# A diffusion trunk on one core: the opening's loads, norm and modulation in another order, and attention's columns and bias tables given out sooner

## The chip, the core and the metric

The kernel runs on one core of a Trainium2 chip. Five engines work side by side, each through its own instructions in order: TensorE (PE, matmuls; PEld is its loading of weights), VectorE (DVE), ScalarE (ACT), GpSimd (POOL) and SyncE (SP), which here only issues transfers. An engine waits where an instruction needs what another engine or a transfer has not yet delivered. The metric is the device time of one execution in microseconds.

## What is computed

Two layers over 512 tokens of width 1024. The first mixes by gated chunks and by neighbourhood attention with 256 context tokens, the second by a convolution; both end with a squared-ReLU MLP. Cut to what the change touches:

```python
sc_c = silu(c); sc_ctx = silu(c_ctx)
for l in range(2):
    m = sc_c @ w_mod[l] + b_mod[l]            # shift, scale, gain for both sub-layers
    sh1, s1, g1, sh2, s2, g2 = split(m, 6)
    h = rmsnorm(x, norm_g[l, 0]) * (1 + s1) + sh1
    if l == 0:
        hc = rmsnorm(ctx, norm_g[0, 0]) * (1 + cs1) + csh1
        z, q, k, v = split(h @ w_in)           # kc, vc from hc
        a = spatial_gating(z)
        b = softmax(q k^T / 8 + bias(rpb), masked) v     # 8 heads, windows of 8 x 16, and context
        y = concat(a, b) @ w_out
    else:
        y = conformer_conv(h)
    x = x + g1 * y
    x = x + g2 * square(relu((rmsnorm(x, norm_g[l, 1]) * (1 + s2) + sh2) @ w1)) @ w2
return rmsnorm(x, final_g)
```

## The kernel before

Activations are kept transposed, 1024 features as eight tiles of 128 x 512 tokens. Large matmuls are done three times in the short fp32r form, as high x high, low x high and high x low (L88, L89, L90, helper `mm3`); ACT casts the high half of each weight and VectorE or GpSimd subtracts to get the low half (`split`, L93 and L94). Results sit in eight PSUM banks that are handed round in order: a matmul into a bank waits until the last reader of that bank is done.

**Opening** (L250 to L500). SyncE issues every load in one queue: cc, four tiles of x (two feature blocks each, L256), vec, kon (L272), the modulation weights wmA (L266) and the first weight blocks raw (L120). ACT makes silu of c and squares eight blocks of x (L378), VectorE adds them one after another (L380), TensorE sums the last one over features in four narrow products (L386), ACT takes the root (L388), VectorE the reciprocal (L389), TensorE spreads it over all partitions (L392) and ACT copies it to r0 (L394). VectorE makes eight 128 x 128 diagonal blocks dgc from silu(c) (L400); TensorE multiplies them by ones (`silu_rows`, L404), and ACT copies the result to cB, the row that the columns below need. `mod_products(f)` for f = 0 to 3 gives shift and scale of two feature blocks each: eight products with wmA (L415), a copy ms (L420), a turn on TensorE (L424), and three small VectorE steps (L429 to L432). `modulate` then forms t = x · gain · r0 on VectorE (L350), the high half t + shift on ACT (L355), the low half on VectorE (L363). `first_operand(f)` calls it for two blocks, and takes a list of deferred low halves of the first weight (L136) to slip in after the first t. The products of the first q and k follow in `first_products`.

**Attention.** The 16 units u (four pairs of heads, four query blocks each) run two at a time: `scores` (three products per head, L831), `soften` (VectorE adds the bias table and finds the minimum, L844; ACT takes exp, L848), `turn` (TensorE turns the weights, L861; ACT copies them, L863) and, one round later, `weigh` (L877; at the last unit of a pair of heads also the sums, L885, the copy rs, L889, and yb, L891). Between these stand fill steps, `more(n)`: the products of values, projections and gate, with a weight piece split by ACT and GpSimd after each.

Beside them VectorE works through 24 columns: `gemv(j)` (L542) multiplies half of a 128 x 2048 tile graw with cB and sums it. The tile is one buffer with two halves, column j in half j mod 2; `early_load(j + 2)` (L527), called right behind column j, has SyncE fetch the half anew. `work(1)` takes one column, and is called four times in each round with u below 12. A bias table of a head is six VectorE additions (`head_bias`, L710) on a strip that `load_bias` fetches by two transfers (L698). The strips of two heads are fetched at the first round of a head pair, and their two tables made in its second round, after the first and third `work`. `turn_v` (L635 to L639) turns the values of one head pair; its two ACT copies vtok stand at the end of rounds 6 and 10. Where nothing else sets it, the order on each engine is that in which the code is written:

```python
        more(1)
        if u < 12:
            work(1)
        more(2)
        turn(u)
        if p_ < 3 and j == 2:
            head_bias(2 * p_ + 2, rows.pop(2 * p_ + 2))
```

Of the kernel before, what the change touches and what calls it, by code (L numbers as in the profile page):

```python
# [55 lines left out]
def body(ctx: ExitStack, tc: tile.TileContext, I: dict, out: bass.AP):  # L56
# [49 lines left out]
    class Weights:  # L106
# [16 lines left out]
        def piece(self, i, q, el=None):  # L123
# [11 lines left out]
            if isinstance(el, list):  # L135
                act.copy(hi.parts[q], src)  # L136
                el.append(lambda: dve.tensor_tensor(lo.parts[q], src, hi.parts[q].bitcast(F32), op=ALU.subtract))
            else:
                split(hi.parts[q], lo.parts[q], src, el=e)
# [113 lines left out]
    for k in range(0, KC, 2):  # L253
        t = mpa.tile([P, 2, 512], F32, tag="ablk", name=nm("x0"), bufs=6)
        x0 += [t[:, 0], t[:, 1]]
        sync.dma_start(t, I["xT"][:, k : k + 2, :])  # L256
# [7 lines left out]
    def load_wmA(i):  # L264
        w = graw() if i == 0 else sp.tile([P, 2048], F32, name=f"wmA{i}")
        sync.dma_start(w, I["wmA"][i])  # L266
        wmA.append(w.rearrange("p (k n) -> p k n", k=4))
# [4 lines left out]
    sync.dma_start(kon[:, :C_MASK], I["kon"][:, :C_MASK])  # L272
# [102 lines left out]
    before = None  # L375
    for k in range(KC):
        sq = slot(s="sq")
        act.activation(sq, x0[k], AF.Square)  # L378
        if k:
            dve.tensor_tensor(sq, sq, before, op=ALU.add)  # L380
        before = sq
    preload(AF.Sqrt)

    ps = bank()[:, :4]
    for n in range(4):
        pe.matmul(ps[:, n : n + 1], before[:, n * P : (n + 1) * P], ones[:, :1], start=True, stop=True)  # L386
    q = small(4, "q")
    act.activation(q, ps, AF.Sqrt, bias=epsc, scale=1.0 / D)  # L388
    dve.reciprocal(q, q)  # L389
    ps = bank()  # L390
    for n in range(4):
        pe.matmul(ps[:, n * P : (n + 1) * P], q[:, n : n + 1].to_broadcast([P, P]), ident, start=True, stop=True)  # L392
    r0 = slot(s="rstd")
    act.copy(r0, ps)  # L394


    cB = cp.tile([P, D], F32, name="cB")
    dgs = [slot(s="dgc") for _ in range(2)]
    for k in range(KC):
        dve.tensor_scalar(dgs[k // 4][:, k % 4 * P : k % 4 * P + P], ident, sc[:, k, 0:1], None, op0=ALU.mult)  # L400

    def silu_rows(i):
        ps = bank()
        pe.matmul(ps, ones, dgs[i], start=True, stop=True)  # L404
        return ps
# [44 lines left out]
    def first_operand(f, low=()):  # L450
        m = modulate([(x0[k], *colA(0, k), h[k][0], h[k][1]) for k in (2 * f, 2 * f + 1)], r0, lambda k: False)
        next(m)
        for go in low:
            go()
        run(m)

    pbs = {}
    pm = mod_products(0)
    next(pm)
    next(pm)  # L460
    next(pm)
    pbs[0] = silu_rows(0)
    run(pm)
    low = []
    W.piece(0, 0, low)
    first_operand(0, low)
# [7 lines left out]
    pbs[1] = silu_rows(1)  # L474
# [4 lines left out]
    for i in range(2):  # L479
        act.copy(cB[:, i * 512 : (i + 1) * 512], pbs[i])  # L480
# [38 lines left out]
    early = []  # L519

    def early_load(j):
# [3 lines left out]
        if j < 24:  # L525
            b = j % 2 * D
            sync.dma_start(early[0][:, b : b + D], I["wmB"][j // 2][:, b : b + D])  # L527
# [10 lines left out]
    def gemv(j):  # L538
# [6 lines left out]
        if j < 22:  # L545
            early_load(j + 2)
# [347 lines left out]
    rows = {hd: load_bias(hd) for hd in range(2)}  # L894
    for n, _ in enumerate(values(0, ctx_first)):
        if n in (6, 8):
            head_bias(n // 2 - 3, rows.pop(n // 2 - 3))
# [25 lines left out]
    def more(n):  # L923
        for _ in range(n):
# [3 lines left out]
            stage(begun)  # L928
            W.pieces(1, pool)


    NU = len(units)
    for u in range(0, NU, 2):
        p_, j = units[u]
        if p_ < 3 and j == 0:
            for e in range(2):
                rows[2 * p_ + 2 + e] = load_bias(2 * p_ + 2 + e)
# [6 lines left out]
        more(1)  # L944
        if u < 12:
            work(1)
        more(2)
        turn(u)
        if p_ < 3 and j == 2:
            head_bias(2 * p_ + 2, rows.pop(2 * p_ + 2))  # L950
        if u < 12:
            work(1)
        more(1)
        turn(u + 1)
        if u < 12:
# [634 lines left out]
```

## Time and profile before

| | us |
|---|---|
| time, median of 3 runs | 1176.74 (1176.14 to 1180.42) |
| the profiled execution | 1178.93 |
| its span in the trace | 1177.0 |
| of that, stretch 0 to 30: PE busy | 13.88 |
| stretch 30 to 75: PE busy | 44.25 of 45.00 |
| stretch 75 to 193 (attention): PE busy | 113.49 of 118.00, at a granted clock of 0.97 |
| stretch 193 to 1177: PE busy | 973.41 of 984.00 |

The profiled execution took 1.93 us more than its span, which runs from the first instruction to the last. Busy time of an engine is the time in which it executes; the granted clock is the share of full speed that TensorE was given. An idle stretch in the trace names what ended it, as in "<-DVE gn L728": the engine waited for the VectorE instruction of line 728 that writes gn.

### The profile page before, as it was taken

How to read it: one execution, taken by the hardware profiler on the slowest of the kernel's cores; microseconds unless marked ns; L12 is line 12 of the kernel's file. 1: busy time of each engine (PE TensorE's matmuls, PEld its weight loads, DVE VectorE, ACT ScalarE, POOL GpSimd, SP SyncE). 2: the span in 40 equal slices, each digit the busy share in tenths (PEclk: the TensorE clock that was granted, in tenths of full speed). 3: DMA queues.
4: the chain of work that ended last, by engine and by line, in shares of the span. 5: the costliest groups of instructions: out<-in, count | busy, mean ns of one | idle time of the engine just before them, and what ended most of it. 6: DMA issues, size and time to landing. Idle time of an engine off the chain costs nothing.

```text
span 1177.0 us, 16486 instructions
## 1 busy us (share of the span) xinstructions
PE 1145.0 (97%) x6574; PEld 954.9 (81%) x6574; DVE 722.1 (61%) x1247; ACT 472.2 (40%) x939; POOL 168.7 (14%) x162
## 2 busy tenths in 40 slices
PE   4999998999999999999999999999999999999997
PEld 2688897889888888888889766699988888888887
DVE  4666876658765665766667868577743443443445
ACT  4463555545532422423336232475632331341423
POOL 0142325552100000000023220043200000000001
PEclk9999998999999999999999999999999999999998
DMA  9525462242455455554531444304222332232322
GB/s 372 222 89 189 149 226 90 73 179 73 161 202 209 182 198 192 196 201 175 214 113 72 131 126 134 111 1 144 72 97 82 108 107 76 104 107 72 108 72 72
DMA packets 31468, 161.89 MB, mean 138 GB/s; under 512 B 4320, under 2 KB 7904, under 8 KB 15008
## 3 DMA queue, kind: packets, MB, share of 16 engines
q1 hardware_dynamic: 31392, 160.85, 39.2%
q8 instruction: 51, 0.84, 0.3%
q14 instruction: 25, 0.20, 0.1%
HBM read 152.52 MB, written 2.10 MB: 131 GB/s over the span
## 4 chain that ended last, share of the span: by engine, by line
PE 86%; DVE 6%; ACT 3%; DMA 3%; issue 1%; POOL 0%; SPq 0%; DVEq 0%; ACTq 0%; POOLq 0%
PE ps L88 22%; PE ps L89 22%; PE ps L90 22%; PE ps L218 3%; PE ps L215 3%; PE ps L216 3%; PE ps L1248 3%; DMA graw<-in_wmB_dram 2%; PE ps L877 1%; DVE graw L542 1%; PE ps L415 1%; DVE acc L325 1%; PE ps L831 1%; ACT s L848 1%; PE ps L861 1%
## 5 line engine op out<-in xcount | busy, mean ns | idle before, releaser
L93 ACT CAST whi<-raw 128x512 fp32r<-128x512 f32 x339 | 190.7, 616 | 197.7 <-PE ps L90 173.2
L88 PE MATMUL ps<-hhi,whi 128*128 128x512 f32 x640 | 251.7, 393 | 1.4 <-ACT hhi L355 1.4
L90 PE MATMUL ps<-hlo,whi 128*128 128x512 f32 x640 | 249.3, 390 | 0.4 <-DVE hlo L363 0.4
L89 PE MATMUL ps<-hhi,wlo 128*128 128x512 f32 x640 | 249.3, 390 | 0.2 <-DVE wlo L94 0.2
L94 DVE TENSOR_TENSOR wlo<-raw,whi 128x512 fp32r<-128x512 f32 x283 | 194.1, 723 | 36.8 <-ACT whi L93 35.9
L89 PE MATMUL ps<-hid,wlo 128*128 128x512 f32 (+1 forms) x520 | 196.3, 378 | 0.0
L90 PE MATMUL ps<-hid,whi 128*128 128x512 f32 (+1 forms) x520 | 196.3, 378 | 0.0
L88 PE MATMUL ps<-hid,whi 128*128 128x512 f32 (+1 forms) x520 | 196.3, 378 | 0.0
L998 DVE SCALAR_TENSOR_TENSOR x<-ps,mod,x 128x512 f32<-128x512 f32 (+1 forms) x94 | 62.7, 669 | 157.1 <-PE ps L90 148.0
L88 PEld LDWEIGHTS ps<-hhi,whi 128*128 128x128 f32 x640 | 120.2, 188 | 32.8 <-issue 6.1
L94 POOL TENSOR_TENSOR wlo<-raw,whi 128x512 fp32r<-128x512 f32 x56 | 81.9, 1479 | 427.0 <-ACT whi L93 426.8
L90 PEld LDWEIGHTS ps<-hlo,whi 128*128 128x128 f32 x640 | 120.1, 188 | 26.1 <-DVE hlo L363 0.9
L89 PEld LDWEIGHTS ps<-hhi,wlo 128*128 128x128 f32 x640 | 120.2, 188 | 24.4 <-DVE wlo L94 0.5
L542 DVE CUSTOM_DVE_ANT_0 graw<-graw,cB,vec 128x1024 f32<-128x1024 f32 x80 | 105.1, 1315 | 17.5 <-DMA graw<-in_wmB_dram 17.5
L88 PEld LDWEIGHTS ps<-hid,whi 128*128 128x128 f32 x520 | 97.8, 188 | 18.2
L90 PEld LDWEIGHTS ps<-hid,whi 128*128 128x128 f32 x520 | 97.8, 188 | 18.2
L89 PEld LDWEIGHTS ps<-hid,wlo 128*128 128x128 f32 x520 | 97.8, 188 | 18.0
L1124 DVE TENSOR_TENSOR z<-z 128x512 f32<-128x512 f32 (+1 forms) x72 | 46.4, 651 | 94.3 <-ACT z L1122 94.2
L1122 ACT ACTIVATE z<-ps 128x512 f32<-128x512 f32 (+1 forms) x72 | 38.9, 550 | 139.3 <-PE ps L90 136.7
L1128 DVE TENSOR_TENSOR hid<-z,hid 128x512 fp32r<-128x512 f32 (+1 forms) x72 | 45.7, 642 | 43.3 <-ACT hid L1126 43.3
L1126 ACT CAST hid<-z 128x512 fp32r<-128x512 f32 (+1 forms) x72 | 40.7, 573 | 51.8 <-DVE z L1124 51.8
L1478 POOL TENSOR_TENSOR o<-o,rstd 128x256 f32<-128x256 f32 x2 | 1.9, 952 | 322.2 <-DVE rstd L336 322.2
(260 smaller groups left out, 1680.1 us busy)
## 6 DMA issues: line engine op xcount, KB each, us to landing
raw<-in_w_ff_dram SPq DMA_DIRECT2D x64, 1024.0 KB
graw<-in_wmB_dram SPq DMA_DIRECT2D x28, 1024.0 KB
graw<-in_wmB_dram SPq DMA_DIRECT2D x24, 512.0 KB
raw<-in_w_pw_dram SPq DMA_DIRECT2D x12, 1024.0 KB
raw<-in_w_in_dram SPq DMA_DIRECT2D x10, 1024.0 KB
wmA<-in_wmA_dram SPq DMA_DIRECT2D x7, 1024.0 KB
y<-ypad SPq DMA_DIRECT2D x90, 67.5 KB
raw<-in_w_out_dram SPq DMA_DIRECT2D x4, 1024.0 KB
```

Source lines behind the costliest of these rows:

```text
L88: pe.matmul(ps, w[0], a[0], start=first, stop=False)
L89: pe.matmul(ps, w[1], a[0], start=False, stop=False)
L90: pe.matmul(ps, w[0], a[1], start=False, stop=last)
L93: (e or act.copy)(hi, src)
L94: (el or dve).tensor_tensor(lo, src, hi.bitcast(F32), op=ALU.subtract)
L215: pe.matmul(ps, w[0][:, k, c : c + P], a[0], start=n == 0, stop=False)
L542: dve.tensor_tensor_reduce(out=wv, in0=wv, in1=cB, scale=1.0, scalar=vcol(V_BMOD, l * 48 + q * 8 + j % 8), op0=ALU.mult, op1=ALU.add, accu ...
L998: dve.scalar_tensor_tensor(x[:, m, t0:t1], ps, gate[:, m : m + 1], x[:, m, t0:t1], op0=ALU.mult, op1=ALU.add)
L1122: act.activation(z, ps, AF.Relu)
L1124: dve.tensor_tensor(z, z, z, op=ALU.mult)
L1126: act.copy(hi, z)
L1128: dve.tensor_tensor(lo, z, hi.bitcast(F32), op=ALU.subtract)
```

## The change

In the opening, ACT's queue issues the second and fourth tile of x, kon and the second wmA; SyncE the rest. VectorE adds the squares in pairs only, and TensorE sums the four pairs over features into one bank, by products with a 128 x 128 matrix of ones, so that root and reciprocal are taken on all 128 partitions by 512 columns and no spreading is needed. GpSimd makes the eight dgc, both products with ones and the copies to cB come ahead of the first `mod_products`. x · r0 is formed ahead of the modulation (`scaled`), and ACT makes the high half from it with scale and shift in one step, VectorE the same in place and the low half from that. The deferral of the weight's low half goes.

In attention, the 24 columns stand as five in each of the rounds u = 0, 2, 4, 6 and four in u = 8, one after each fill step from the first on; u = 10 has none. The reload of a half is put on a list when its column is given out, and issued by ACT's queue after two more fill steps. One bias table is made in every round up to u = 10 (`next_bias`, after the third fill step), and the strip of the head two further on is fetched right behind it.

```diff
--- before.py
+++ after.py
@@ -132,11 +132,7 @@
             hi, lo = self.his[i]
             e = (dve, pool)[q % 2] if el == "both" else el
             src = self.raws[i][:, 2 * q : 2 * q + 2, :]
-            if isinstance(el, list):
-                act.copy(hi.parts[q], src)
-                el.append(lambda: dve.tensor_tensor(lo.parts[q], src, hi.parts[q].bitcast(F32), op=ALU.subtract))
-            else:
-                split(hi.parts[q], lo.parts[q], src, el=e)
+            split(hi.parts[q], lo.parts[q], src, el=e)
             self.cut += 1
             if q == 3:
                 del self.raws[i]
@@ -253,7 +249,7 @@
     for k in range(0, KC, 2):
         t = mpa.tile([P, 2, 512], F32, tag="ablk", name=nm("x0"), bufs=6)
         x0 += [t[:, 0], t[:, 1]]
-        sync.dma_start(t, I["xT"][:, k : k + 2, :])
+        (act if k % 4 else sync).dma_start(t, I["xT"][:, k : k + 2, :])
     st = ExitStack()
     sp = st.enter_context(tc.tile_pool(name="start", bufs=1))
     wmA = []
@@ -263,13 +259,13 @@
     def load_wmA(i):
         w = graw() if i == 0 else sp.tile([P, 2048], F32, name=f"wmA{i}")
-        sync.dma_start(w, I["wmA"][i])
+        (act if i == 1 else sync).dma_start(w, I["wmA"][i])
         wmA.append(w.rearrange("p (k n) -> p k n", k=4))
     vec = cp.tile([P, NV], F32, name="vec")
     sync.dma_start(vec, I["vec"])
     kon = cp.tile([P, NC_], F32, name="kon")
-    sync.dma_start(kon[:, :C_MASK], I["kon"][:, :C_MASK])
+    act.dma_start(kon[:, :C_MASK], I["kon"][:, :C_MASK])
     load_wmA(0)
     load_wmA(1)
     W.load()
@@ -372,37 +368,29 @@
     sc = blk(s="sc")[:, : KC * 32].rearrange("p (k m) -> p k m", m=32)
     act.activation(sc, cc, AF.Silu)
-    before = None
+    ss = SumSq()
+    ss.ps = bank()
+    dgs = [slot(s="dgc") for _ in range(2)]
     for k in range(KC):
         sq = slot(s="sq")
         act.activation(sq, x0[k], AF.Square)
-        if k:
+        if k % 2:
             dve.tensor_tensor(sq, sq, before, op=ALU.add)
+            pe.matmul(ss.ps, ones, sq, start=k == 1, stop=k == KC - 1)
         before = sq
+    cB = cp.tile([P, D], F32, name="cB")
+    for k in range(KC):
+        pool.tensor_scalar(dgs[k // 4][:, k % 4 * P : k % 4 * P + P], ident, sc[:, k, 0:1], None, op0=ALU.mult)
     preload(AF.Sqrt)
-    ps = bank()[:, :4]
-    for n in range(4):
-        pe.matmul(ps[:, n : n + 1], before[:, n * P : (n + 1) * P], ones[:, :1], start=True, stop=True)
-    q = small(4, "q")
-    act.activation(q, ps, AF.Sqrt, bias=epsc, scale=1.0 / D)
-    dve.reciprocal(q, q)
-    ps = bank()
-    for n in range(4):
-        pe.matmul(ps[:, n * P : (n + 1) * P], q[:, n : n + 1].to_broadcast([P, P]), ident, start=True, stop=True)
-    r0 = slot(s="rstd")
-    act.copy(r0, ps)
-    cB = cp.tile([P, D], F32, name="cB")
-    dgs = [slot(s="dgc") for _ in range(2)]
-    for k in range(KC):
-        dve.tensor_scalar(dgs[k // 4][:, k % 4 * P : k % 4 * P + P], ident, sc[:, k, 0:1], None, op0=ALU.mult)
-    def silu_rows(i):
+    r0 = ss.rstd(0, T)
+    pbs = []
+    for d in dgs:
         ps = bank()
-        pe.matmul(ps, ones, dgs[i], start=True, stop=True)
-        return ps
+        pe.matmul(ps, ones, d, start=True, stop=True)
+        pbs.append(ps)
+    for i in range(2):
+        act.copy(cB[:, i * 512 : (i + 1) * 512], pbs[i])
@@ -447,23 +435,25 @@
                 w, c = wqk[n // 2], (n % 2) * P
                 mm3(q0[n], (w[0][:, k, c : c + P], w[1][:, k, c : c + P]), h[k], k == 0, k == KC - 1)
-    def first_operand(f, low=()):
-        m = modulate([(x0[k], *colA(0, k), h[k][0], h[k][1]) for k in (2 * f, 2 * f + 1)], r0, lambda k: False)
-        next(m)
-        for go in low:
-            go()
-        run(m)
-    pbs = {}
+    def scaled(f):
+        for k in (2 * f, 2 * f + 1):
+            dve.tensor_tensor(x0[k], x0[k], r0, op=ALU.mult)
+    def first_operand(f):
+        for k in (2 * f, 2 * f + 1):
+            gs, sh = colA(0, k)
+            hi, lo = h[k]
+            act.activation(hi, x0[k], AF.Identity, scale=gs, bias=sh)
+            dve.tensor_scalar(x0[k], x0[k], gs, sh, op0=ALU.mult, op1=ALU.add)
+            dve.tensor_tensor(lo, x0[k], hi.bitcast(F32), op=ALU.subtract)
+        if f < 3:
+            scaled(f + 1)
+    scaled(0)
     pm = mod_products(0)
-    next(pm)
-    next(pm)
-    next(pm)
-    pbs[0] = silu_rows(0)
     run(pm)
-    low = []
-    W.piece(0, 0, low)
-    first_operand(0, low)
+    W.piece(0, 0)
+    first_operand(0)
     for q in range(1, 4):
         W.piece(0, q)
     wqk = {0: W.use()}
@@ -471,13 +461,10 @@
     pm = mod_products(1)
     next(pm)
     next(pm)
-    pbs[1] = silu_rows(1)
     next(pm)
     W.piece(1, 0)
     run(pm)
     first_operand(1)
-    for i in range(2):
-        act.copy(cB[:, i * 512 : (i + 1) * 512], pbs[i])
     for q in range(1, 4):
         W.piece(1, q)
     ctile = []
@@ -516,7 +503,7 @@
     gpool = [None, 12]
     gs_ = ExitStack()
-    early = []
+    early, soon = [], []
     def early_load(j):
@@ -524,7 +511,7 @@
             early.append(graw())
         if j < 24:
             b = j % 2 * D
-            sync.dma_start(early[0][:, b : b + D], I["wmB"][j // 2][:, b : b + D])
+            act.dma_start(early[0][:, b : b + D], I["wmB"][j // 2][:, b : b + D])
     def gemv_load(i):
         if i < 40:
@@ -543,7 +530,7 @@
             out=wv, in0=wv, in1=cB, scale=1.0, scalar=vcol(V_BMOD, l * 48 + q * 8 + j % 8),
             op0=ALU.mult, op1=ALU.add, accum_out=mods[(l, q)][:, j % 8 : j % 8 + 1])
         if j < 22:
-            early_load(j + 2)
+            soon.append([2, lambda: early_load(j + 2)])
         elif j == 23:
             gemv_load(gpool[1])
             gpool[1] += 1
@@ -892,9 +879,15 @@
             yb[p_] = b
     rows = {hd: load_bias(hd) for hd in range(2)}
+    def next_bias(hd):
+        head_bias(hd, rows.pop(hd))
+        if hd < 6:
+            rows[hd + 2] = load_bias(hd + 2)
     for n, _ in enumerate(values(0, ctx_first)):
         if n in (6, 8):
-            head_bias(n // 2 - 3, rows.pop(n // 2 - 3))
+            next_bias(n // 2 - 3)
         if n > 7:
             W.pieces(1, pool)
     early_load(0)
@@ -926,40 +919,34 @@
             if next(fill, 1) is None:
                 nfill[0] += 1
             stage(begun)
+            for due in list(soon):
+                due[0] -= 1
+                if due[0] == 0:
+                    due[1]()
+                    soon.remove(due)
             W.pieces(1, pool)
     NU = len(units)
+    columns = {0: 5, 2: 5, 4: 5, 6: 5, 8: 4}
     for u in range(0, NU, 2):
         p_, j = units[u]
-        if p_ < 3 and j == 0:
-            for e in range(2):
-                rows[2 * p_ + 2 + e] = load_bias(2 * p_ + 2 + e)
         left = [scores(u), scores(u + 1)]
         if u >= 2:
             weigh(u - 2)
             weigh(u - 1)
         left[0]()
         left[1]()
-        more(1)
-        if u < 12:
-            work(1)
-        more(2)
-        turn(u)
-        if p_ < 3 and j == 2:
-            head_bias(2 * p_ + 2, rows.pop(2 * p_ + 2))
-        if u < 12:
-            work(1)
-        more(1)
-        turn(u + 1)
-        if u < 12:
-            work(1)
-        if p_ < 3 and j == 2:
-            head_bias(2 * p_ + 3, rows.pop(2 * p_ + 3))
-        more(2)
-        if u < 12:
-            work(1)
-        more(1)
+        for n in range(7):
+            more(1)
+            if n == 2:
+                turn(u)
+            if n == 3:
+                turn(u + 1)
+            if n < columns.get(u, 0):
+                work(1)
+            if n == 2 and p_ < 3:
+                next_bias(2 * p_ + 2 + j // 2)
         if u in (6, 10):
             later.popleft()()
     weigh(NU - 2)
```

Three places show what this moves. Rows give line, operation, tiles and shape, and what is waited for (an engine's name stands for its semaphore, DMAHW for a transfer). First TensorE's beginning, before: sq are the squares, ps PSUM banks, graw and wmA the modulation weights.

```order
L386 MATMUL ps_142<-ones,sq_137 128x1 [waits DVE_49,Pool_49]
L386 MATMUL ps_142<-ones,sq_137 128x1 x3
L392 MATMUL ps_150<-kon,q_147 128x128 [waits DMAHW6_49,DVE_49]
L392 MATMUL ps_150<-kon,q_147 128x128 x3
L415 MATMUL ps_188<-graw_89,sc_115 32x512 [waits DMAHW7_49,Activation_49]
L415 MATMUL ps_188<-graw_89,sc_115 32x512 x3
L415 MATMUL ps_188<-wmA_91,sc_115 32x512 [waits DMAHW0_49]
L415 MATMUL ps_188<-wmA_91,sc_115 32x512 x3
L424 MATMUL ps_199<-kon,ms_197 128x128 [waits Activation_49]
L424 MATMUL ps_199<-kon,ms_197 128x128 x3
L404 MATMUL ps_204<-dgc_158,ones 128x512 [waits DVE_49]
```

And now:

```order
L379 MATMUL ps_117<-sq_122,ones 128x512 [waits DVE_49,Pool_49]
L379 MATMUL ps_117<-sq_128,ones 128x512 [waits DVE_49]
L379 MATMUL ps_117<-sq_134,ones 128x512 [waits DVE_49]
L379 MATMUL ps_117<-sq_140,ones 128x512 [waits DVE_49]
L390 MATMUL ps_158<-dgc_118,ones 128x512 [waits Pool_49]
L390 MATMUL ps_160<-dgc_119,ones 128x512 [waits Pool_49]
L403 MATMUL ps_186<-graw_89,sc_115 32x512 [waits DMAHW0_49,Activation_49]
L403 MATMUL ps_186<-graw_89,sc_115 32x512 x3
L403 MATMUL ps_186<-wmA_91,sc_115 32x512 [waits DMAHW7_49]
L403 MATMUL ps_186<-wmA_91,sc_115 32x512 x3
L412 MATMUL ps_197<-kon,ms_195 128x128 [waits DMAHW6_49,Activation_49]
L412 MATMUL ps_197<-kon,ms_195 128x128 x3
```

The four narrow sums and the spreading (L386, L392) have become four sums by 512 columns, and the two products with dgc, which stood behind the turn and in the second round, stand ahead of the first modulation product and wait for GpSimd.

Second, ACT's last rows of round u = 6, before: pt are turned attention weights, whi weight pieces, qt a projection, vtok the turned values, rs the spread sums.

```order
L863 COPY pt_1350<-ps_1345 128x512 [waits PE_49,Activation_49]
L863 COPY pt_1357<-ps_1352 128x512 [waits PE_49,Activation_49]
L93 CAST whi_1333<-raw_845 128x512
L863 COPY pt_1381<-ps_1376 128x512 [waits PE_49,Activation_49]
L863 COPY pt_1388<-ps_1383 128x512 [waits PE_49,Activation_49]
L583 ACTIVATE qt_1404<-ps_1326 128x8x8x8 [waits PE_49]
L93 CAST whi_1333<-raw_845 128x512
L638 COPY vtok_1428<-ps_1429 128x512 [waits PE_49]
L639 COPY vtok_1428<-ps_1430 128x384 [waits PE_49]
L889 COPY rs_1488<-ps_1479 128x512 [waits PE_49]
```

And now, with the transfers that ACT issues:

```order
L514 DMA graw_780<-in_wmB_dram 128x1024 [waits DMAHW2_49,DVE_49]
L93 CAST whi_1337<-raw_834 128x512
L850 COPY pt_1390<-ps_1385 128x512 [waits PE_49,Activation_49]
L850 COPY pt_1397<-ps_1392 128x512 [waits PE_49,Activation_49]
L570 ACTIVATE qt_1406<-ps_1330 128x8x8x8 [waits PE_49]
L514 DMA graw_780<-in_wmB_dram 128x1024 [waits DMAHW5_49,DVE_49]
L93 CAST whi_1337<-raw_834 128x512
L514 DMA graw_780<-in_wmB_dram 128x1024 [waits DMAHW6_49,DVE_49]
L514 DMA graw_780<-in_wmB_dram 128x1024 [waits DMAHW0_49,DVE_49]
L625 COPY vtok_1432<-ps_1433 128x512 [waits PE_49]
L626 COPY vtok_1432<-ps_1434 128x384 [waits PE_49]
L876 COPY rs_1486<-ps_1477 128x512 [waits PE_49]
```

Four of the five reloads of the round stand in these rows, and the last two directly ahead of the vtok copies, each waiting for a VectorE instruction, the column that frees the half.

Third, VectorE in round u = 10, before: gelu and gn belong to the gate, biases are the tables, graw the columns.

```order
L725 SCALAR_TENSOR_TENSOR gelu_1755<-gelu_1755,ps_1721 128x256 [waits Activation_49]
L710 TENSOR_TENSOR biases<-rows_1440,kon 128x128 [waits DMAHW2_49,DMAHW1_49]
L710 TENSOR_TENSOR biases<-rows_1440,kon 128x128 x5
L542 ISA graw_784,mod_414<-graw_784,cB,vec 128x1024 [waits DMAHW2_49]
L542 ISA mod_414 128x1
L728 SCALAR_TENSOR_TENSOR gn_1754<-gelu_1755,ps_1721 128x256 [waits Activation_49]
L761 BN_STATS bs_1795<-gn_1754 128x6 [waits DVE_49]
L762 BN_AGGR gmv<-bs_1795 128x2 [waits DVE_49]
L761 BN_STATS bs_1798<-gn_1754 128x6
L762 BN_AGGR gmv<-bs_1798 128x2 [waits DVE_49]
L856 RECIPROCAL tot_1446<-tot_1446 128x8
L542 ISA graw_784,mod_414<-graw_784,cB,vec 128x1024 [waits DMAHW4_49]
```

And now:

```order
L712 SCALAR_TENSOR_TENSOR gelu_1757<-gelu_1757,ps_1723 128x256 [waits Activation_49]
L697 TENSOR_TENSOR biases<-rows_1372,kon 128x128 [waits DMAHW4_49,DMAHW3_49]
L697 TENSOR_TENSOR biases<-rows_1372,kon 128x128 x5
L715 SCALAR_TENSOR_TENSOR gn_1756<-gelu_1757,ps_1723 128x256 [waits Activation_49]
L748 BN_STATS bs_1795<-gn_1756 128x6 [waits DVE_49]
L749 BN_AGGR gmv<-bs_1795 128x2 [waits DVE_49]
L748 BN_STATS bs_1798<-gn_1756 128x6
L749 BN_AGGR gmv<-bs_1798 128x2 [waits DVE_49]
L843 RECIPROCAL tot_1444<-tot_1444 128x8
L712 SCALAR_TENSOR_TENSOR gelu_1829<-gelu_1829,ps_1780 128x256 [waits Activation_49]
L715 SCALAR_TENSOR_TENSOR gn_1828<-gelu_1829,ps_1780 128x256 [waits Activation_49]
L748 BN_STATS bs_1834<-gn_1828 128x6 [waits DVE_49]
```

The columns are gone from this round, and of its two bias tables one is left.

## The prediction

> **What bounds the kernel now.** I read the page's busy times first, then TensorE's waits, then windows, then the chain and the timeline at the places found. Page, lines of busy time (share of the span, instructions); below it TensorE's waits (what waited, for whom: us in total, times, the longest):
>
> ```profile
> span 1177.0 us, 16486 instructions
> PE 1145.0 (97%) x6574; PEld 954.9 (81%) x6574; DVE 722.1 (61%) x1247; ACT 472.2 (40%) x939; POOL 168.7 (14%) x162
> PE ps L386 <- DVE sq L380: 13.0, 1, 13.0
> PE ps L831 <- DVE gn L728: 4.3, 1, 4.3
> PE ps L331 <- DVE acc L325: 1.5, 2, 0.9
> ```
>
> TensorE is the bound: 1177.0 − 1145.0 = 32 us are all that it is idle. Thirteen are the start and 4.3 are one wait in attention, so a change that leaves the matmuls alone works on some 20 us. Windows (start:end, length, then busy time and count on PE, PEld, DVE, ACT and POOL, granted clock, DMA share, GB/s):
>
> ```profile
> 0.00:10.00 10.00, 0.00 (x0) 0.00 (x0) 2.32 (x4) 5.14 (x8) 0.49 (x7) 1.00 0.80 268
> 10.00:20.00 10.00, 6.47 (x32) 4.16 (x32) 4.25 (x13) 3.49 (x6) 0.00 (x0) 1.00 1.02 428
> 181.00:188.00 7.00, 6.99 (x55) 6.07 (x56) 2.53 (x8) 1.87 (x6) 5.82 (x5) 0.54 0.47 154
> ```
>
> The third row shows a second cost of that one wait: the 7.00 us behind it ran at a granted clock of 0.54 with TensorE never idle, 7.00 × (1 − 0.54) = 3.2 us of work lost.
>
> **The stall in attention, which goes.** Timeline around it (start, duration, engine, line; in brackets idle before and its releaser; SPq is a DMA issue on SyncE's queue):
>
> ```profile
> 171.07 0.33 SPq L120 DMA_DIRECT2D raw<-in_w_in_dram  x1
> 171.49 2.77 SPq L527 DMA_DIRECT2D graw<-in_wmB_dram  x2
> 177.21 1.29 DVE L542 CUSTOM_DVE_ANT_0 graw<-graw,cB,vec 128x1024 f32<-128x1024 f32 x1 [1.95 <-DMA graw<-in_wmB_dram]
> 178.42 1.30 DVE L710 TENSOR_TENSOR biases<-rows,kon 128x128 f32<-128x128 f32 x6
> 180.54 0.42 DVE L728 SCALAR_TENSOR_TENSOR gn<-gelu,ps 128x256 f32<-128x256 f32 x1 [0.48 <-ACT gelu L727]
> 181.01 0.79 PE L831 MATMUL ps<-kh,q 64*128 64x512 f32 x1 [4.27 <-DVE gn L728]
> ```
>
> Read backwards: the scores wait for the bank that a gate product (L728) empties; VectorE does that late, behind a bias table and a column that waits 1.95 for its half, which SyncE issued behind a weight block. The new order puts no column into u = 10 and one bias table instead of two: columns (2 to 3 × 1.29), a bias (1.30) and the DMA wait (1.95) leave that row, 5.8 at least where 4.27 is needed. So the wait of 4.27 and the half clock of 3.2 go: **−7.5**. Late next there is the ready-made row of softmax work, which TensorE reaches with no wait in the pairs before; I cost it at 0.
>
> **The opening.** Chain of waits, in order of time (start, duration, step), and below it rows of the timeline and of groups (busy, mean ns):
>
> ```profile
> 12.13 0.70 DVE sq L380
> 17.45 3.25 PE ps L415 x16
> 20.72 0.59 ACT ms L420
> 21.36 0.67 PE ps L424 x4
> 22.05 0.20 DVE modA L429
> 24.76 0.67 DVE hlo L363
> 25.48 0.50 PE ps L90
> 28.08 1.90 PE ps L415 x16
> 10.12 1.15 ACT L378 ACTIVATE sq<-x 128x512 f32<-128x512 f32 x2 [0.17 <-DMA x<-in_xT_dram]
> 21.85 1.02 PE L404 MATMUL ps<-dgc,ones 128*128 128x512 f32 x2
> L336 DVE RECIPROCAL rstd<-rstd x8: 1753/1753/1754, 58.7 to 1160.1; 128x256 f32<-128x256 f32 x8
> L779 POOL TENSOR_SCALAR gn<-gn,gmv,gsd 128x128 f32<-128x128 f32 x8 | 6.3, 791 | 0.0
> L1213 DVE TENSOR_SCALAR zc<-ypad,vec 128x512 f32<-128x512 f32 x2 | 1.1, 539 | 0.0
> 136.34 6.10 POOL L94 TENSOR_TENSOR wlo<-raw,whi 128x512 fp32r<-128x512 f32 x4 [13.08 <-ACT whi L93]
> ```
>
> Two paths now meet at the first operand; both start when the squares are done. In the kernel before, two squares after the last tile end at 10.12 + 1.15 = 11.27 and the adds at 12.83. Now tiles 1 and 3 come by ACT's queue; the engines were 80% busy until 10 and more than full behind it, so tiles 2 and 3 land together at 10: four squares, 4 × 0.575, end at 12.3, one add (0.70) at 13.0. No gain there.
>
> Path one, 1/rms by 512 columns: the last sum 1.0 (the L404 row; up to 1.7 at the 3.25/1.90 that L415 shows cold over warm), root 0.6, reciprocal 2 × 1753 ns = 3.5, two products with x at 0.70: 13.0 + 1.0 + 0.6 + 3.5 + 1.4 = 19.5, 20.2 cold. Path two: GpSimd makes the eight dgc from the third add on, about 11.7. No row shows this operation there: the bounds per piece are 0.38 (L94, 6.10/16 blocks of 128 columns) and 0.79 (L779, same shape, two arithmetic steps where dgc has one); L779 is nearer by shape, L94 by steps, and I take the middle, 0.58: 11.7 + 4.7 = 16.4, second ones product 17.4, L403's eight products at 1.90 to 3.25, say 2.5: 19.9. Then, as in before, ms 0.59, turn 0.67, three small DVE steps of 0.20; then hi 0.58 on ACT, straight from x, DVE's 0.54 and 0.67: 3.7, and 0.3 for hand-overs: L90 at 23.9 against 25.48, a gain of 1.6. With 0.79 and 3.25 it is 26.4, a loss of 0.9; with 0.38 and 1.90 path one decides: 20.2 + 0.2 + 0.58 + 0.54 + 0.67 = 22.2, a gain of 3.3. The two cB copies and the weight's low half, which stood in the chain's holes, are still there and beside other work. The next operands lose a DVE product each (x · rstd is done ahead); of the 1.5 us waits at L331 I let 0.5 go. **−2.1**, between +0.9 and −3.8.
>
> The share of 0.80 up to 10 us leaves room the other way: 20% of 10 us were unused, and if a second queue filled them, x would land up to 2.0 us sooner and the opening give 4.1. Against it stands the same row: one queue alone reached 1.02 as soon as large tiles stood in it, so the engines and not the issue set the pace; I leave the 2.0 out. The Trainium skill, "DMA: Bandwidth & Descriptors", section "Issuing engines are not separate DMA queues", says that transfers run on the same 16 engines whichever engine starts them, and that a second issuer saves only sequencer time. By that rule the split tiles bring nothing and the sum stays at 1175.0; without it, it would be 1173.0.
>
> **The new wait.** Columns are five per pair in u = 0 to 6 instead of four, over the same two halves. ACT's queue now issues each half, two fill steps after the column that freed it. Timeline, queue and VectorE, then TensorE and ACT:
>
> ```profile
> 104.89 0.33 SPq L527 DMA_DIRECT2D graw<-in_wmB_dram  x1
> 108.61 1.28 DVE L542 CUSTOM_DVE_ANT_0 graw<-graw,cB,vec 128x1024 f32<-128x1024 f32 x1 [1.21 <-DMA graw<-in_wmB_dram]
> 109.82 3.47 DVE L710 TENSOR_TENSOR biases<-rows,kon 128x128 f32<-128x128 f32 x6
> 131.77 0.69 DVE L844 CUSTOM_DVE_ANT_1 s<-ps,biases 128x512 f32<-128x512 f32 x1
> 136.12 1.27 DVE L542 CUSTOM_DVE_ANT_0 graw<-graw,cB,vec 128x1024 f32<-128x1024 f32 x1
> 137.32 5.68 DVE L710 TENSOR_TENSOR biases<-rows,kon 128x128 f32<-128x128 f32 x6
> 142.18 0.59 ACT L638 COPY vtok<-ps 128x512 f32<-128x512 f32 x1 [1.94 <-PE ps L635]
> 145.79 1.04 PE L885 MATMUL ps<-kon,tot 128*64 128x128 f32 x16
> 146.62 0.42 DVE L93 CAST q<-qt 128x512 fp32r<-128x512 f32 x1
> 147.07 0.69 DVE L94 TENSOR_TENSOR q<-qt,q 128x512 fp32r<-128x512 f32 x1
> 160.77 2.31 DVE L542 CUSTOM_DVE_ANT_0 graw<-graw,cB,vec 128x1024 f32<-128x1024 f32 x1 [1.07 <-DMA graw<-in_wmB_dram]
> ```
>
> A half takes 108.61 − 104.89 = 3.7 from issue to use, a column 1.28: 5.0 per turn of a half, while three of a pair's five columns wait for a turn within it. ACT does its rows in order, so at each L514 it holds everything behind it until that column has run. In pair u = 6 those behind five L514 are the two vtok copies (L625, L626), and TensorE's L872 waits for the bank that L625 empties. Worked forward: the softens began at 131.77; pair 4, one column fuller, puts them later by an estimated 1.0, so 132.8. The first column starts 136.12 − 131.77 = 4.35 behind them and takes 1.3 (138.45); its half again 3.7 (142.15), third column 1.3 (143.45), bias table 1.30 alone or 5.68 beside GpSimd (144.75 to 149.1), fourth column 1.3, q's cast and low half 0.42 + 0.69 (147.15 to 151.5), last column 1.3 (148.45 to 152.8), issue 0.33 and the copy 0.59: 149.4 to 153.7. TensorE was at L885 at 145.79: it is 3.6 to 7.9 us late, **+5.7** in the middle (part of it at the transposes before). If the loads arrive ahead of need it is 0; a gain has no source there, since TensorE waited for nothing in those pairs. Later pairs have four columns and none; nothing is left over.
>
> **Sum**, against the profiled execution's own 1178.93 (span 1177.0 and 1.93 around it; the median shown is 1176.74, so 2.2 lower): 1178.93 − 7.5 − 2.1 + 5.7 = **1175.0**. About 0.5% (5.9 us) is what a measurement of this kernel can tell from no change; this is −0.15%, the same.
>
> The Trainium skill, "TensorE: Matmul & The Clock Gate", section "Why this matters for your kernels", warns of gaps over some 3 us, after which TensorE is throttled to half. The row at 181 agrees; by it the new wait, if it is one piece, would cost a stretch at half clock again. That gives rival D below.
>
> **The rivals.**
> A: nothing is given back. For it: the queue of SyncE no longer stands between column and half, and ACT is only 40% busy. Against it: ACT's in-order row, and 3.7 + 1.3 twice in a pair. 1178.93 − 7.5 − 2.1 = 1169.3.
> B, slower: VectorE beside GpSimd. GpSimd's split (6.10 at 136.34) stretched a bias table from 1.30 to 5.68 and elsewhere to 3.47, and a column to 2.31; every pair now has a bias. If pair 4's table takes 2.2 more and two columns 1.0 more each on top of the upper 7.9, the wait is 12.1, and with another half-clock stretch (3.2): 1178.93 − 7.5 − 2.1 + 12.1 + 3.2 = 1184.6. It decides from a loss of 13.3 on. Against it: GpSimd is busy 14% of the span.
> C: the opening does not do what it says, GpSimd's dgc being as slow as 0.79 and L403 cold: 1178.93 − 7.5 + 5.7 = 1177.1.
> D: the wait before L872 comes in one piece above 4 us, and the half clock with it: 1175.0 + 3.2 = 1178.2. For it is the row at 181. Against: the three runs of before lie 4.3 apart (1176.14 to 1180.42), so such a stretch is not in every execution.
>
> **How the numbers follow.** Forecast 0.40, A 0.23, C 0.12, D 0.16, B 0.09. The range reaches from A with the opening's best, 1178.93 − 7.5 − 3.8 = 1167.6, to D with the wait's upper end and the opening's half microsecond, 1178.93 − 7.5 − 0.5 + 7.9 + 3.2 = 1182.0; it leaves out B and a tenth beside. Below 1170.9 are A and a few hundredths of the forecast's: faster 0.26. Above 1182.6 is B, most of it: slower 0.08. Same 0.66.
>
> **What would show it.** Right: no TensorE wait above 1 us at the scores near 177, granted clock 1.00 from 181 to 188; first L90 at 23 to 25; gaps on VectorE in front of columns in u = 4 and 6 that end with a graw DMA, ACT's vtok copy at 149 or later, and a TensorE wait of 3 to 6 us before L872 or the transposes near it. Wrong: vtok copied near 142 with TensorE busy throughout (then A), GpSimd's L384 above 0.7 a piece (C), granted clock near 0.5 after 150 (D), bias tables of 5 us in two pairs (B).

## The result and the profile after

The changed kernel takes 1182.45 us (median of 20 runs, 1179.67 to 1185.54), the one before 1177.41 (20 runs, 1175.08 to 1180.85): a ratio of 1.0036, 95% interval 1.0026 to 1.0045. It is slower by 4 to 5 us, where 1175.0 was predicted, with a range of 1167.6 to 1182.0. The profiled execution took 1184.13 us.

The page's busy times and TensorE's waits of the changed kernel, in the same form as above:

```profile
span 1182.3 us, 16462 instructions
PE 1148.7 (97%) x6566; PEld 954.0 (81%) x6566; DVE 723.3 (61%) x1244; ACT 474.0 (40%) x938; POOL 172.4 (15%) x170
PE ps L379 <- DVE sq L378: 9.5, 1, 9.5
PE ps L872 <- ACT vtok L625: 4.5, 1, 4.5
PE ps L848 <- ACT s L835: 3.6, 3, 2.5
PE ps L327 <- DVE acc L321: 1.6, 2, 0.8
```

The first wait is shorter since TensorE now sums early, not since the opening is. The wait of the scores for the gate's bank is gone. In its place stand L872's wait for the vtok copy, named in the prediction, and waits of L848, the turn of the attention weights, for exp. TensorE's busy time grew by 3.7 us with slightly fewer instructions: it ran slower somewhere. Windows show where (columns as before; the clock is the third number from the end):

```profile
22.00:24.00 2.00, 1.12 (x3) 0.68 (x4) 1.69 (x4) 2.00 (x5) 0.00 (x0) 0.75 1.01 418
24.00:26.00 2.00, 2.00 (x6) 1.52 (x6) 1.97 (x5) 0.51 (x1) 0.00 (x0) 0.50 1.02 426
26.00:28.00 2.00, 2.00 (x6) 1.24 (x4) 1.75 (x3) 0.00 (x0) 0.00 (x0) 0.50 1.02 426
28.00:30.00 2.00, 2.00 (x13) 0.52 (x16) 0.00 (x0) 0.00 (x0) 0.00 (x0) 0.54 0.97 406
150.00:158.00 8.00, 3.50 (x48) 3.10 (x48) 5.54 (x13) 1.59 (x3) 1.27 (x1) 0.88 0.79 238
158.00:166.00 8.00, 8.00 (x41) 6.61 (x38) 6.04 (x14) 4.55 (x11) 0.00 (x0) 0.69 0.41 152
174.00:182.00 8.00, 8.00 (x85) 7.80 (x84) 5.81 (x24) 5.58 (x16) 2.56 (x2) 1.00 0.57 199
```

Two stretches at half clock: one behind L872's wait, and one in the opening, where the kernel before had 1.00 throughout. Around 181, where the old stall was, nothing is left. Timeline of the opening on TensorE and GpSimd, then the two long waits, each with the rows on VectorE or ACT that lead to it (ACTq is a DMA issue on ACT's queue):

```profile
16.44 1.12 PE L390 MATMUL ps<-dgc,ones 128*128 128x512 f32 x2 [0.81 <-POOL dgc L384]
20.12 0.66 PE L412 MATMUL ps<-kon,ms 128*128 128x128 f32 x4 [0.71 <-ACT ms L408]
22.31 0.50 PE L88 MATMUL ps<-hhi,whi 128*128 128x512 f32 x1 [1.53 <-ACT hhi L446]
23.62 0.80 PE L90 MATMUL ps<-hlo,whi 128*128 128x512 f32 x1 [0.57 <-DVE hlo L448]
24.21 0.63 PE L88 MATMUL ps<-hhi,whi 128*128 128x512 f32 x1
11.51 4.88 POOL L384 TENSOR_SCALAR dgc<-kon,sc 128x128 f32<-128x128 f32 x8 [10.49 <-DVE sq L378]
134.76 1.28 DVE L529 CUSTOM_DVE_ANT_0 graw<-graw,cB,vec 128x1024 f32<-128x1024 f32 x1 [3.19 <-DMA graw<-in_wmB_dram]
138.51 0.68 DVE L831 CUSTOM_DVE_ANT_1 s<-ps,biases 128x512 f32<-128x512 f32 x1
140.16 1.36 PE L848 MATMUL ps<-kon,s 128*128 128x128 f32 x8 [2.49 <-ACT s L835]
153.34 2.60 ACTq L514 DMA_DIRECT2D graw<-in_wmB_dram  x2
155.99 0.59 ACT L625 COPY vtok<-ps 128x512 f32<-128x512 f32 x1 [5.12 <-DVE mod L529]
156.63 1.97 PE L872 MATMUL ps<-kon,tot 128*64 128x128 f32 x16 [4.50 <-ACT vtok L625]
```

The vtok copy stands behind two loads on ACT's queue, and the second of them was issued only after the column that frees its half had run: ACT stood idle for 5.12 us, and L872 waited 4.50.

L90 starts at 23.62 instead of 25.48, 1.86 sooner; then each product takes 0.63 instead of some 0.40. The account of the two profiled executions: the old stall and its half clock −7.5, the opening −1.9, its lost clock 2 × 0.25 + 2 × 0.50 + 2 × 0.50 + 2 × 0.46 = +3.4, waits in attention +8.1 (2.49, 4.50 and two of 1.1 together), the clock behind them 8 × 0.12 + 8 × 0.31 = +3.4 at most, since TensorE was idle in part of the first of these windows: +5.5, where 1184.13 − 1178.93 = 5.2.

### The profile page after: what moved, and what is told of

It is laid out like the page before. It is cut to its first block, busy times and chain, and to the rows that moved or that the text cites. A ratio compares the mean times of both kernels' runs of the same rounds, so it can differ in the third digit from the quotient of the medians.

```text
span 1182.3 us, 16462 instructions
## 1 busy us (share of the span) xinstructions
PE 1148.7 (97%) x6566; PEld 954.0 (81%) x6566; DVE 723.3 (61%) x1244; ACT 474.0 (40%) x938; POOL 172.4 (15%) x170
## 4 chain that ended last, share of the span: by engine, by line
PE 86%; DVE 6%; DMA 4%; ACT 3%; issue 1%; POOL 1%; ACTq 0%; DVEq 0%; SPq 0%; POOLq 0%
PE ps L88 22%; PE ps L90 22%; PE ps L89 22%; PE ps L214 3%; PE ps L211 3%; PE ps L212 3%; PE ps L1235 3%; DMA graw<-in_wmB_dram 3%; DVE graw L529 1%; DVE acc L321 1%; PE ps L403 1%; PE ps L735 1%; ACT s L835 1%; PE ps L736 1%; PE ps L737 1%
## 5 line engine op out<-in xcount | busy, mean ns | idle before, releaser
L88 PE MATMUL ps<-hhi,whi 128*128 128x512 f32 x640 | 253.4, 396 | 1.5 <-ACT hhi L446 1.5
L90 PE MATMUL ps<-hlo,whi 128*128 128x512 f32 x640 | 251.0, 392 | 0.6 <-DVE hlo L448 0.6
L90 PE MATMUL ps<-hid,whi 128*128 128x512 f32 (+1 forms) x520 | 196.3, 378 | 0.0
L88 PE MATMUL ps<-hid,whi 128*128 128x512 f32 (+1 forms) x520 | 196.3, 378 | 0.0
L88 PEld LDWEIGHTS ps<-hhi,whi 128*128 128x128 f32 x640 | 121.1, 189 | 32.8 <-issue 5.4
L90 PEld LDWEIGHTS ps<-hlo,whi 128*128 128x128 f32 x640 | 121.1, 189 | 26.4 <-DVE hlo L448 1.0
L88 PEld LDWEIGHTS ps<-hid,whi 128*128 128x128 f32 x520 | 97.9, 188 | 18.2
L90 PEld LDWEIGHTS ps<-hid,whi 128*128 128x128 f32 x520 | 97.9, 188 | 17.9
```

What stands on the lines that cost most here:

```text
L88: pe.matmul(ps, w[0], a[0], start=first, stop=False)
L90: pe.matmul(ps, w[0], a[1], start=False, stop=last)
```

## The experiments

In each, the ratio is to the kernel before, run in the same rounds on the same chip.

**The two halves of the change apart.** The opening as changed with the attention of before, and the reverse:

> The changed opening with the attention of before. Theory one (the opening's gain is eaten by a half-clock stretch that follows the holes at 19 to 22 us): first L90 near 23.6 as in the changed kernel, granted clock near 0.5 from about 23 to 30 us, the 4.27 us wait at the scores near 177 still there; 1 to 2 us slower than before, ratio 1.001. Rival (the stretch belongs to that one profile, not to the opening): granted clock 1.00 up to 75 us and 1.5 to 2 us faster than before, ratio 0.9985.

> The opening of before with the changed attention. Theory one (attention gives back more than the stall was worth): L848 waits some 2.5 us and L872 some 4.5 us, half clock behind the latter, the wait near 177 gone: 3 to 5 us slower than before, ratio 1.003 to 1.004. Rival (most of the loss came from the opening): at most 1.5 us slower, ratio up to 1.0013.

The opening alone: 1179.48, ratio 1.0006 (0.9996 to 1.0017). The attention alone: 1181.47, 1.0022 (1.0011 to 1.0033). So the opening brings nothing that these runs resolve, and the attention costs; together they make some 1.003. The opening's profile shows the clock again, and the attention's its waits (first a window, then two rows of TensorE's waits):

```profile
22.00:30.00 8.00, 6.65 (x20) 3.97 (x24) 6.34 (x12) 3.07 (x5) 0.00 (x0) 0.57 1.01 422
...
PE ps L861 <- ACT s L848: 5.1, 3, 2.7
PE ps L885 <- ACT vtok L638: 4.5, 1, 4.5
```

**The hole in the opening.** The holes around the turn are not new. Before, they were 0.71 and 1.43 us long, and the clock stayed at 1.00 (a window, then two rows of the kernel before):

```profile
20.00:30.00 10.00, 7.42 (x43) 3.34 (x36) 5.76 (x11) 4.10 (x7) 0.00 (x0) 1.00 1.02 424
21.36 0.66 PE L424 MATMUL ps<-kon,ms 128*128 128x128 f32 x4 [0.71 <-ACT ms L420]
24.30 0.50 PE L88 MATMUL ps<-hhi,whi 128*128 128x512 f32 x1 [1.43 <-ACT hhi L355]
```

But one product with dgc followed the turn at 21.85, so that 1.5 us of work stood between the two holes. The change moved it ahead: the 0.66 us of the turn is all that is left between holes of 0.7 and 1.5 to 1.9. One run fills the second with a product whose result is not used, the other puts the two products back there:

```diff
     run(pm)
+    pe.matmul(bank(), ones, dgs[0], start=True, stop=True)
     W.piece(0, 0)
```

> The changed opening with the attention of before, and one product with ones more (about 1 us, its result unused) behind TensorE's first turn, in the hole of 1.5 to 1.9 us ahead of the first operand. Theory one (the hole lets the clock drop in part of the executions, and that eats the opening's gain): granted clock 1.00 from 22 to 30 us, 1.5 to 2.5 us faster than the changed opening alone, ratio to before 0.998 to 0.999. Rival (the drop comes from elsewhere, or costs little): ratio within 0.0005 of the 1.0006 of the changed opening alone.

```diff
     run(pm)
+    for d in dgs:
+        ps = bank()
+        pe.matmul(ps, ones, d, start=True, stop=True)
+        pbs.append(ps)
     W.piece(0, 0)
```

> The changed opening with the attention of before, but the two products with dgc put behind the first turn, and the copies to cB behind the second operand, as before the change. Theory one: the products fill the hole and no longer wait for GpSimd ahead of the first modulation product; first L90 at 23.0 to 23.8, granted clock 1.00 from 22 to 30 us, ratio to before 0.998 to 0.999. Rival: the two products run into the first operand's time and L88 begins 0.5 to 1 us later than the 22.31 of the changed kernel; ratio 1.000 or more.

With the filler 1176.61, 0.999 (0.9978 to 1.0002); the two products in the hole 1178.07, 0.9995 (0.9983 to 1.0007). The filler's profile, window and first operand:

```profile
22.00:30.00 8.00, 6.20 (x34) 3.13 (x34) 6.16 (x11) 3.60 (x7) 0.00 (x0) 1.00 1.01 421
...
22.29 0.50 PE L88 MATMUL ps<-hhi,whi 128*128 128x512 f32 x1 [0.67 <-ACT hhi L446]
23.60 0.50 PE L90 MATMUL ps<-hlo,whi 128*128 128x512 f32 x1 [0.58 <-DVE hlo L448]
```

L90 stands where it stood, at 23.60, and the products behind it run at full clock. The times alone only hint at it, since the intervals touch; the mean granted clock of each execution says it. Over the eleven runs of the opening alone it was 0.991 to 0.994, median 0.992; over the twelve with the filler 0.994 to 0.997, median 0.995. Eight of the eleven lie below all twelve. The difference of 0.003 of 1177 us is some 3.5 us of full clock, about one such stretch, so in this kernel it is lost in most executions. In the other filling L88 came at 22.87 and L90 at 24.18, since the last sum over features ended at 16.0 there instead of 14.8, and so part of the gain was missing.

An open hole does not always bring the drop. Seven of the kernels profiled here have the changed opening with the hole left open. In five the clock fell (0.57 from 22 to 30 us in three, 0.79 in two); in two it stayed at 1.00: the two next below, in which SyncE issues the columns' loads, the first of them at 80 us or later. Here is the one with SyncE at once, a window and TensorE's wait before the first operand:

```profile
22.00:30.00 8.00, 6.07 (x33) 3.12 (x33) 6.17 (x11) 3.96 (x7) 0.00 (x0) 1.00 1.02 425
PE ps L88 <- ACT hhi L446: 1.9, 1, 1.9
```

All three profiles with the filler show 1.00, and so does the other filling, whose hole behind the two products was still 1.91 long. So the clock was kept more often with work behind the turn, but the length of the hole alone does not settle it in a single execution. The same holds in attention: the wait of 2.49 in the changed kernel was followed by full clock (L848 took 1.36), one of 2.17 in a kernel below was not (1.82). What decides it stays open.

**Who issues the columns' loads, and when.** Three kernels: SyncE with the delay, SyncE at once, ACT at once.

```diff
-            act.dma_start(early[0][:, b : b + D], I["wmB"][j // 2][:, b : b + D])
+            sync.dma_start(early[0][:, b : b + D], I["wmB"][j // 2][:, b : b + D])
```

> The changed kernel with the columns' loads issued by SyncE, still two fill steps later. Theory one (ACT's rows wait behind the loads): L872's wait of 4.50 us goes with the half clock behind it, 3.0 us or so; L848's 2.49 us stays in part: 5 to 8 us faster than the changed kernel, 1174.5 to 1177.5. Rival (two halves are too few for five columns, whoever issues): TensorE waits 6 us or more in attention as in the changed kernel, within 2 us of its 1182.45.

```diff
-            soon.append([2, lambda: early_load(j + 2)])
+            early_load(j + 2)
```

> The changed kernel with the columns' loads issued by SyncE directly behind the column that frees the half, as before the change; five columns a round and one bias table a round stay. Theory one: no TensorE wait above 1 us in attention, 9 to 12 us faster than the changed kernel, 1170.5 to 1173.5. Rival (two halves are too few): VectorE still waits 3 us for halves in rounds 4 and 6, L848 or L872 wait over 2 us, 1176 or more.

> The changed kernel with the columns' loads still issued by ACT, but directly behind the column that frees the half instead of two fill steps later. Theory one (what costs is that a waiting load holds up ACT's row): ACT now stands still for every column, TensorE's waits in attention reach 12 us or more, 1186 or more. Rival (the delay of two steps is what costs, the queue is not): VectorE's waits for halves shrink as with SyncE, 1175 to 1178.

SyncE with the delay: 1203.22, 1.0203 (1.0185 to 1.0221), both theories missed by far. SyncE at once: 1175.73, 0.9976 (0.9967 to 0.9986), faster than both kernels; it lies between the two theories, just below the rival's 1176, and waits above 1 us are left. ACT at once: 1184.4, 1.0045 (1.003 to 1.0059), with waits of 8.3 us in attention where the changed kernel has 8.1: neither theory's number came, and on ACT's row the delay makes no difference that these runs resolve. The last two kernels differ in the issuer alone, so the 8 to 9 us between them come from issuing these loads on ACT's queue: in the profiles 8.3 us of waits against 3.3, and over the executions a median mean clock of 0.992 against 0.996. The failure with SyncE and the delay in its timeline, SyncE's queue and VectorE:

```profile
97.56 1.30 DVE L697 TENSOR_TENSOR biases<-rows,kon 128x128 f32<-128x128 f32 x6
98.89 1.29 SPq L685 DMA_DIRECT2D rows<-in_rpb_dram  x2
100.22 0.91 SPq L514 DMA_DIRECT2D graw<-in_wmB_dram  x2
105.10 1.28 DVE L529 CUSTOM_DVE_ANT_0 graw<-graw,cB,vec 128x1024 f32<-128x1024 f32 x1 [6.24 <-DMA graw<-in_wmB_dram]
```

The strip of the head two further on (L685) waits until the bias table has been made, and the delay had put the column's load behind it in SyncE's row. At once, the load stands ahead of the strip. What is left of the waits for exp then is 3.0 us in three, the longest 1.3, against 8.1 with ACT.

Why ACT is the wrong place shows in the changed kernel already in round 4, not only at vtok (ACT's queue, ACT and VectorE):

```profile
115.94 2.27 DVE L529 CUSTOM_DVE_ANT_0 graw<-graw,cB,vec 128x1024 f32<-128x1024 f32 x1 [1.18 <-DMA graw<-in_wmB_dram]
118.26 0.33 ACTq L514 DMA_DIRECT2D graw<-in_wmB_dram  x1
118.63 0.62 ACT L93 CAST whi<-raw 128x512 fp32r<-128x512 f32 x1 [2.84 <-DVE mod L529]
119.16 0.58 ACT L876 COPY rs<-ps 128x512 f32<-128x512 f32 x1
119.77 0.69 DVE L878 TENSOR_TENSOR yb<-ps,rs 128x512 f32<-128x512 f32 x1 [1.55 <-ACT rs L876]
120.38 0.68 DVE L831 CUSTOM_DVE_ANT_1 s<-ps,biases 128x512 f32<-128x512 f32 x1
```

The load at 118.26 had to wait for the column that ended at 118.21; the copy rs stood behind it, yb behind rs on VectorE, and the softens behind yb, at 120.38. With SyncE at once, rs was copied at 115.44 and the softens began at 116.75; of these 3.6 us, 1.6 came from the round before, since TensorE's sums (L872) began at 115.97 instead of 114.35:

```profile
115.44 0.59 ACT L876 COPY rs<-ps 128x512 f32<-128x512 f32 x1 [5.70 <-PE ps L872]
116.75 0.67 DVE L831 CUSTOM_DVE_ANT_1 s<-ps,biases 128x512 f32<-128x512 f32 x1
```

**The vtok copies ahead of the last loads.**

```diff
+            if n == 3 and u in (6, 10):
+                later.popleft()()
-        if u in (6, 10):
-            later.popleft()()
```

> The changed kernel with the turn of the values (L625, L626) given out three fill steps sooner in rounds 6 and 10, so that its copies stand ahead of the round's last two loads in ACT's row. Theory one (ACT's rows wait behind the loads): L872's wait of 4.50 us goes with the half clock behind it, the waits of L848 stay: 4 to 7 us faster than the changed kernel, 1175.5 to 1178.5. Rival (VectorE is late by itself, whatever ACT does): the wait moves to L848 of the next round, at most 2 us faster.

1180.31, 1.0018 (1.0007 to 1.0029): L872's wait went, and L848's grew from 3.6 to 6.2 us. The rival was the nearer: the lateness moved to the next wait. The copy rs now stood behind the same two loads, with ACT idle for 5.13 us ahead of it, and the softens and exp of the next round came after rs.

**Four columns in each of six rounds**, or only the columns taken out of round 10, with all else as before:

```diff
-    columns = {0: 5, 2: 5, 4: 5, 6: 5, 8: 4}
+    columns = {0: 4, 2: 4, 4: 4, 6: 4, 8: 4, 10: 4}
```

> The changed kernel with four columns in each of six rounds instead of five in four and four in one; loads still issued by ACT two fill steps later, one bias table a round. Theory one (the fifth column overruns the two halves): L848's waits under 1 us, L872's under 2 us; of the wait of before near 177 at most 2 us come back since round 10 has columns again: 4 to 7 us faster than the changed kernel, 1175.5 to 1178.5. Rival (the delay and ACT's row cost it, not the count): waits of 5 us or more in rounds 2 to 8 stay, 1180 or more.

```diff
-        if u < 12:
+        if u < 10:
             work(1)
...
         more(1)
+        if u < 8:
+            work(1)
```

> The kernel before, with its queues, opening and bias tables, and only the columns given out as 5, 5, 5, 5 and 4, none in round 10. Theory one (the columns of round 10 alone make the 4.27 us wait and the half clock behind it): that wait under 1 us, 2 to 4 us of waits elsewhere, 2 to 4 us faster than before, ratio 0.9965 to 0.9985. Rival (the two bias tables in round 10 keep the wait): L831 near 177 waits over 2 us, ratio 0.999 or more.

Four columns: 1183.6, 1.0044 (1.0027 to 1.0061). The old stall is back whole although a table fewer is made in round 10, and L872 still waits 2.3:

```profile
PE ps L818 <- DVE gn L715: 4.6, 1, 4.6
PE ps L872 <- ACT vtok L625: 2.3, 1, 2.3
```

Only the columns moved: 1179.25, 1.001 (1.0 to 1.0019), the rival's time. The wait near 177 is gone, as the first theory had it; but round 6, with five columns and two tables, now has one of 5.36 us, and half clock behind it (VectorE, then TensorE):

```profile
153.21 1.28 DVE L542 CUSTOM_DVE_ANT_0 graw<-graw,cB,vec 128x1024 f32<-128x1024 f32 x1 [3.15 <-DMA graw<-in_wmB_dram]
156.67 1.97 PE L861 MATMUL ps<-kon,s 128*128 128x128 f32 x8 [5.36 <-ACT s L848]
```

So the columns of round 10 made the old stall, and taking them out pays only where the round that gets them has room: fewer tables in it, and loads that come at once.

**Put together.** SyncE at once and the filler; and beside that the columns spread:

> The changed kernel with the loads issued by SyncE at once, and the one product more that fills TensorE's hole in the opening. Theory one (both findings add up): granted clock 1.00 from 22 to 30 us in the profile, waits at L848 near 3 us, 1173.5 to 1175, ratio 0.996 to 0.997. Rival (the drop in the opening is rare without the queue of ACT, so that the filler brings nothing): 1175.5 to 1176.5, ratio 0.9975 or more.

```diff
-    columns = {0: 5, 2: 5, 4: 5, 6: 5, 8: 4}
+    columns = {0: 5, 2: 5, 4: 4, 6: 4, 8: 4, 10: 2}
```

> As the last one, with the columns spread as 5, 5, 4, 4, 4 and 2 over the six rounds. Theory one (five columns overrun the two halves): the waits at L848 go below 1.5 us in total and round 12's scores wait under 1 us, as round 10 has two columns and one table: 1 to 2 us faster than with 5, 5, 5, 5 and 4. Rival (any column in round 10 brings the old wait back): L818 near 177 waits over 2 us, slower by 1 us or more.

The first 1175.01, 0.9967 (0.9956 to 0.9979), at the upper edge of the first theory; against SyncE at once alone (1175.73) the filler's share is not resolved, and the mean clocks are close too (median 0.997 of seven executions, 0.996 of eleven without it). The second 1172.86, 0.995 (0.9937 to 0.9963), 5 us faster than the kernel before and 10 faster than the changed one. Its waits in attention are these four, 1.7 us in all:

```profile
103.13 1.36 PE L849 MATMUL ps<-kon,s 128*128 128x128 f32 x8 [1.02 <-ACT s L836]
135.04 1.36 PE L849 MATMUL ps<-kon,s 128*128 128x128 f32 x8 [0.18 <-ACT s L836]
147.26 1.09 PE L873 MATMUL ps<-kon,tot 128*64 128x128 f32 x16 [0.26 <-DVE tot L844]
177.81 0.49 PE L819 MATMUL ps<-kh,q 64*128 64x512 f32 x1 [0.21 <-DVE gn L716]
```

Two columns in round 10 cost 0.21 here. Four cost 4.6 above, but with the loads on ACT's queue, and 4.27 in the kernel before, with a bias table more; the count alone was not varied.

## Why the prediction was wrong

**The stall that goes (−7.5)** was right in cause and size: no wait near 177, clock 1.00. The cause is shown: taking only the columns out of round 10 removed the wait, and four columns there brought it back.

**The opening (−2.1)** was right as far as it went: L90 predicted at 23.9, measured at 23.62; GpSimd's dgc taken at 0.58, measured at 4.88 for eight, 0.61; the load split taken at nothing. That one figure came so near is partly luck, for L90 lay between 23.6 and 24.6 in the seven profiles of this opening. The step that failed is the sum made at an unchanged clock. It counted the product with dgc as work moved, and did not ask what its absence does to what follows. In the profiled execution the half clock there took 3.4 us and turned −1.9 into +1.5. The prediction had seen half clock behind a single wait of 4.27; here it came behind holes of 0.71, 1.53 and 0.57 with short work between. With the filler no profile showed it, without it five of seven did: that the thinner work behind the turn makes the drop likelier is supported by this and by the mean clocks, but why two executions escaped stays open.

**The new wait (+5.7)** had the right mechanism and the right place: ACT's in-order row, vtok, L872. The sum put the first soften of round 6 at 132.8, one microsecond late; it came at 138.51, after a column that waited 3.19 for its half. The step at fault is that 1.0 for "pair 4, one column fuller": it counted the column and left out what ACT's loads hold up on the way: rs, and so yb and the softens, were 3.6 us late already in round 4 (120.38 against 116.75 with SyncE). The waits were 8.1 in sum instead of 5.7.

**The half clock behind the wait** was rival D, at 0.16. The wait of 4.50 came in one piece and brought it, 3.4 at most where 3.2 was priced. Against it the prediction held that the runs of before were 4.3 apart, and so the stretch not in every execution; that told only how often, and a likeliest case that holds a wait above 4 us has to carry a share of it. The waits' 2.4, the two half clocks' 3.4 each and 0.2 of the opening make 9.4; between 1175.0 and the profiled 1184.13 lie 9.1.

B came only in part: the bias tables of rounds 4 and 6 took 1.29 each, clear of GpSimd, but three columns of round 6 took 2.04 to 2.31. C did not come: the opening lost its gain in another way. That the tiles of x split over two queues bring nothing held: the eight squares ended at 7.45 + 4.27 = 11.72, against 11.27 before. This agrees with the Trainium skill, "DMA: Bandwidth & Descriptors", section "Issuing engines are not separate DMA queues", by which a second issuer saves only the time of issuing.

## What to carry to other kernels

A transfer issued by an engine that also computes is an instruction of that engine's row: whatever it waits for, all behind it waits for too (vtok by 5.12 us here), and moving it or its victim in the row only chose other victims (8.1 us of waits in attention with the delay, 8.3 without, 6.2 with vtok put ahead). Before moving work out from between two idle stretches of TensorE, look at what that work does there: in the opening alone a filler of 1 us went with 0.003 more mean clock, an estimated 3.5 us. Work taken from an overfull round has to be counted again in the round that receives it, with its loads.

## What was not expected

TensorE's clock fell to half behind holes none of which was longer than 1.6 us (0.71, 1.53, 0.57, with 1.4 us of work between). With one product of 1.0 us in the longest of them all three profiles stayed at 1.00, and with the attention of before the mean clock of the executions was 0.003 higher; yet two profiles with the hole open stayed at 1.00 as well. A load put later into SyncE's row cost 27 us (1203.22 against 1175.73 at once): the two transfers of a strip, which wait for a bias table, then stood ahead of it.
